# A token mixer's opening with the scale applied first, on TensorE and VectorE, and its output kept by tokens

## The chip, the cores and the metric

One NeuronCore of a Trainium2 chip runs the whole program. The metric is the device time of one execution in microseconds (us); less is better. The kernel before takes 1472.46 us, the median of three runs (1472.07 to 1472.56).

## The reference, cut to what matters

Two transformer blocks work on 256 tokens of width 1024, all in float32. The change touches the first block's way into its token mixer and the way out of it:

```python
ada = jax.nn.silu(c) @ w_ada[l] + b_ada[l]
sh1, sc1, g1, sh2, sc2, g2 = jnp.split(ada, 6, axis=-1)
h = modulate(rms_norm(x, norm1_pre[l]), sh1, sc1)      # h*(1+scale)+shift
y = token_mixer(h, w_in[l], ...)
x = x + g1[:, None, :] * rms_norm(y, norm1_post[l])
h = modulate(rms_norm(x, norm2_pre[l]), sh2, sc2)
y = peer(h, peer_wq[l], peer_subkeys[l], peer_u[l], peer_v[l])
```

In the mixer `proj = h @ w_in` is split into q, k, v, gates and others; q and k go through a causal convolution of four taps and a silu. An RMS norm multiplies each token by one number, the scale multiplies each feature by one number, and the shift adds one number per feature.

## The kernel before, in words

Activations lie by features: `x[128, 8, 256]` has 8 blocks of 128 features, with 256 tokens in the free dimension. Every float32 product is made of three matmuls on rounded halves: `split` (L157) turns 1024 columns of raw weights into a high part `wh` (copy on ScalarE, L165) and a low part `wl` (subtraction, L166, on VectorE or GpSimd). An output block of 128 features takes 24 matmuls of 256 columns: for 8 input blocks, high by high, high by low, low by high (`gemm`, L194). Plain float32 matmuls (fills, sums, transposes) appear as two matmul rows each.

**The opening** follows a hand-written string, `ORD` (L24), one letter per 512 KB load on SyncE's queue. C makes the row `crow` of silu(c) on all partitions; X loads x, sums its squares, and multiplies it by the norm into `u` (L529). Each B (shift) and S (scale) takes a block of `w_ada` and makes 128 numbers of `ada` by one VectorE multiply-and-sum over 1024 columns (`product`, L446). B0 to B7 come first, then S0 to S7; after each S, `A1` is formed (L549), ScalarE applies scale and shift (L551) and rounds to `hh` (L555), and GpSimd makes the low part `hl`. W0 to W5 are the weights of six of the eight q and k blocks. When an `hh` block is there, `some` (L568) runs the matmuls of four outputs (L573); two more outputs follow, and the last two (W6, W7) are loaded in the next list.

**The next list**, `ORD2` (L25): w loads and splits a weight of q or k, q makes its product, u reads one output (`unit_qk`, L600: copy out of PSUM, four taps on VectorE, tanh, gate), v makes a quarter of v (`wide`, L199), l and g the gates. `PV` and `WG` name the splits that GpSimd does. Then a loop over 8 blocks (from L740) makes three products each (`wcxb`) and in their shadow the eight heads, which need the q and k outputs, and two of the later `ada` products each. The program is ordered by priority in the order written, as operands come free, by a planner with its own cost estimates; products of `ada` and the opening's loads keep the order written.

**The mixer's end** (from L826): `acc_k` adds up the output by features in four PSUM banks; then come the squares (ScalarE and VectorE), sums and norm over partitions (L846 to L849), `residual` (L357) with two VectorE operations of 256 columns per block, `scaled` (L338), and the first four products of the next stage (`gemms`, L222). `LA` and `F1` place weight splits and fill matmuls there. **The end of the expert stage** (L1145 to L1182) does the same job by tokens: `acc_tok` (L249) keeps 128 tokens by 512 features per bank, `ended` norms each half with a number per partition, and 16 transposes bring it back.

`NW` (L35) paces the making of expert weights (`weights_of`, L1061) beside the products z 50 to 95; what is left is drained before the next stage starts.

Of the kernel before, what the change touches and what calls it, by code (L numbers as in the profile page):

```python
# [32 lines left out]
LA = ('nnre',(2,3))  # L33
# [5 lines left out]
NZ, NR, NW, ZR, NX, NY = (7, 1.7, 1.4, 50, 1.05, 1.05)  # L39
# [73 lines left out]
def body(ctx: ExitStack, tc: tile.TileContext, a: dict):  # L113
# [243 lines left out]
    def residual(pool_, x, y, r, gain, then=None):  # L357
        for j in range(8):
            u = pool_.tile([128, 256], F32, tag="u", name="u", bufs=2)
            V.scalar_tensor_tensor(out=u, in0=y[:, j, :], scalar=gain[:, j:j + 1], in1=r, op0=ALU.mult, op1=ALU.mult)  # L360
            V.tensor_add(x[:, j, :], x[:, j, :], u)
            if then:
                then(j)
# [68 lines left out]
    with ExitStack() as p1:  # L432
# [3 lines left out]
        crow = m1.tile([128, 1024], F32, name="crow")  # L436
        A.dma_start(out=col, in_=a["cols"])
# [29 lines left out]
        u = big("u", 5)  # L467
        qz = big("qz", 2)
        G.memset(qz, 0.0)
# [9 lines left out]
        banks = [bank(t) for t in ("sc", "num", "den", "ssq", "bc")]  # L479
        psb = bank("psb")  # L480

        early = []

        def load_c():

            c1, t1 = m1.tile([128, 1024], F32, tag="adas", name="c1", bufs=1)[:1], slot_of("t1", 7)[:1, :1024]
            tc.keep_in_program_order(SY.dma_start(out=c1, in_=a["c"]))
            A.activation(t1, c1, AF.Tanh, scale=0.5)
            V.scalar_tensor_tensor(out=c1, in0=t1, scalar=1.0, in1=c1, op0=ALU.add, op1=ALU.mult)
            for n in range(F0):  # L490
                T.matmul(psb[:, :128], lhsT=ones, rhs=ones, start=True, stop=True)
            for i in range(2):
                early[:] = [T.matmul(banks[i], lhsT=ones[:1, :], rhs=c1[:, i * 512:(i + 1) * 512], start=True, stop=True)]
                A.copy(crow[:, i * 512:(i + 1) * 512], banks[i])
# [28 lines left out]
        def load_x():  # L523
            tc.keep_in_program_order(SY.dma_start(out=x, in_=a["xT"].rearrange("p (j t) -> p j t", j=8)))
            with tc.issue_after(early[0].ins):
                sums(m1, banks[4], x, presum(m1, x))
                r1 = norm(m1, banks[4])[0]
# [1035 lines left out]
```

## Time and profile before

| | us |
|---|---|
| median of three runs | 1472.46 |
| the profiled execution | 1472.34 |
| its span in the profile | 1470.3 |
| TensorE busy in the span | 1428.5 |
| VectorE busy | 1152.7 |
| ScalarE busy | 913.8 |
| GpSimd busy | 41.9 |

The profile is of one execution; 2.0 us lie outside its span. TensorE rows are modelled with their pipeline, so a row's length is longer than the pitch at which matmuls follow one another; the pitch is read from start to start. PE is TensorE, PEld its weight loads, DVE is VectorE, ACT is ScalarE, POOL is GpSimd, SP is SyncE.

### The profile page before, as it was taken

What the parts mean: (1) busy time and instruction counts of PE and PEld (TensorE: products, weight loads), DVE (VectorE), ACT (ScalarE), POOL (GpSimd) and SP (SyncE); (2) the same over time, 40 slices, a digit from 0 to 9 for tenths busy, and PEclk for the clock granted to TensorE, in tenths of its full rate; (3) what the DMA queues carried; (4) which work ended last, traced back from release to release, by engine and by line L of the source; (5) the groups of instructions that cost most, each with busy time, mean ns of one, the idle gap of its engine ahead of it and who ended that gap; (6) DMA issues with size and microseconds to landing.
All of it is one profiled execution on the core that took longest, in us unless ns stands there. A gap on an engine that the chain in (4) does not pass through costs nothing.

```text
span 1470.3 us, 27107 instructions
## 1 busy us (share of the span) xinstructions
PE 1428.5 (97%) x10998; PEld 1312.4 (89%) x10998; DVE 1152.7 (78%) x2184; ACT 913.8 (62%) x1288; POOL 41.9 (3%) x30
## 2 busy tenths in 40 slices
PE   5899999999999999999999999999999999999998
PEld 4889999988999999998779997777788899998897
DVE  8988997667999977878999897888855769565554
ACT  3554565446444578887777777787744679554542
POOL 3310000010000000000000000000000000000000
PEclk7999999999999999999999999999999999999999
DMA  9557686453545554453455545555555554255552
GB/s 348 185 190 268 234 345 225 170 171 128 194 151 201 175 178 167 170 172 129 162 173 198 170 151 189 180 173 172 172 176 197 190 171 133 99 193 181 172 174 84
DMA packets 40016, 268.67 MB, mean 183 GB/s; under 512 B 4562, under 2 KB 5330, under 8 KB 9171
## 3 DMA queue, kind: packets, MB, share of 16 engines
q1 hardware_dynamic: 38882, 264.67, 52.0%
q10 hardware_dynamic: 1008, 2.27, 0.5%
q8 instruction: 86, 1.41, 0.4%
q14 instruction: 40, 0.32, 0.1%
HBM read 265.87 MB, written 1.05 MB: 182 GB/s over the span
## 4 chain that ended last, share of the span: by engine, by line
PE 89%; DVE 6%; ACT 3%; DMA 2%; issue 1%; SPq 0%; DVEq 0%; ACTq 0%
PE mm L189 15%; PE mm L191 15%; PE mm L190 15%; PE acc L260 10%; PE acc L261 10%; PE acc L262 10%; PE g L1094 3%; DMA araw<-in_wada_dram 2%; DVE wl L166 1%; PE acc L189 1%; PE acc L191 1%; PE acc L190 1%; ACT wh L165 1%; DVE scr L448 1%; PE mm L225 1%
## 5 line engine op out<-in xcount | busy, mean ns | idle before, releaser
L165 ACT CAST wh<-raw 128x1024 fp32r<-128x1024 f32 x450 | 471.3, 1050 | 428.8 <-PE mm L190 218.4
L166 DVE TENSOR_TENSOR wl<-raw,wh 128x1024 fp32r<-128x1024 f32 x440 | 536.7, 1222 | 161.1 <-ACT wh L165 155.7
L189 PE MATMUL mm<-hh,wh 128*128 128x256 f32 x1816 | 517.4, 285 | 0.0
L191 PE MATMUL mm<-hh,wl 128*128 128x256 f32 x1816 | 511.7, 282 | 0.0
L190 PE MATMUL mm<-hl,wh 128*128 128x256 f32 x1816 | 510.1, 281 | 0.0
L189 PEld LDWEIGHTS mm<-hh,wh 128*128 128x128 f32 x1816 | 342.2, 188 | 2.2
L190 PEld LDWEIGHTS mm<-hl,wh 128*128 128x128 f32 x1816 | 342.8, 189 | 1.0
L191 PEld LDWEIGHTS mm<-hh,wl 128*128 128x128 f32 x1816 | 343.1, 189 | 0.1
L260 PE MATMUL acc<-wh,ah 128*128 128x512 f32 x512 | 205.5, 402 | 0.0
L261 PE MATMUL acc<-wh,al 128*128 128x512 f32 x512 | 202.6, 396 | 0.0
L262 PE MATMUL acc<-wl,ah 128*128 128x512 f32 x512 | 202.3, 395 | 0.0
L1072 ACT COPY o<-os 128x1024 f16<-128x1024 f16 x96 | 197.0, 2052 | 0.2 <-DVE os L1069 0.2
L262 PEld LDWEIGHTS acc<-wl,ah 128*128 128x128 f32 x512 | 96.7, 189 | 22.5
L261 PEld LDWEIGHTS acc<-wh,al 128*128 128x128 f32 x512 | 96.6, 189 | 20.8
L260 PEld LDWEIGHTS acc<-wh,ah 128*128 128x128 f32 x512 | 96.2, 188 | 20.7
L1097 DVE SCALAR_TENSOR_TENSOR z<-g,z 128x256 f32<-128x256 f32 x128 | 51.3, 422 | 44.9 <-PE g L1094 44.4
L1069 DVE TENSOR_TENSOR os<-io,idxT 128x1024 f16<-128x1024 f16 x96 | 66.4, 692 | 25.2 <-ACT o L1072 24.8
L1079 DVE TENSOR_TENSOR og<-o,gT 128x512 f16<-128x512 f16 (+1 forms) x96 | 82.7, 861 | 0.1
L1094 PEld LDWEIGHTS <-o 128*128 128x128 f16 x1536 | 46.4, 96 | 17.6 <-issue 11.9
L448 DVE SCALAR_TENSOR_TENSOR scr<-araw,crow 128x1024 f32<-128x1024 f32 x48 | 60.5, 1260 | 0.9 <-DMA araw<-in_wada_dram 0.6
L1094 PE MATMUL g<-og,o 128*128 128x32 f16 (+1 forms) x1536 | 56.5, 182 | 2.4 <-ACT o L1072 2.4
L268 DVE TENSOR_TENSOR al<-z,ah 128x256 fp32r<-128x256 f32 x128 | 53.5, 420 | 3.1 <-ACT ah L267 3.1
(437 smaller groups left out, 1888.1 us busy)
## 6 DMA issues: line engine op xcount, KB each, us to landing
raw<-in_uT_dram SPq DMA_DIRECT2D x64, 1024.0 KB, 4.9
raw<-in_ev_dram SPq DMA_DIRECT2D x64, 1024.0 KB, 4.9
araw<-in_wada_dram SPq DMA_DIRECT2D x16, 1024.0 KB, 5.2
raw<-in_wup_dram SPq DMA_DIRECT2D x16, 1024.0 KB, 4.9
raw<-in_wdn_dram SPq DMA_DIRECT2D x16, 1024.0 KB, 5.0
raw<-in_wcxb_dram SPq DMA_DIRECT2D x12, 1024.0 KB, 5.1
araw<-in_wada_dram SPq DMA_DIRECT2D x16, 512.0 KB, 9.8
raw<-in_wout_dram SPq DMA_DIRECT2D x8, 1024.0 KB, 4.9
```

The source lines that it names most:

```text
L165: by.copy(wh, raw) if by is A else by.tensor_copy(wh, raw)
L166: last = on.tensor_sub(wl, raw, wh)
L189: T.matmul(ps, lhsT=wh, rhs=xh, start=start, stop=False, skip_group_check=skip)
L190: T.matmul(ps[:, :n], lhsT=wh, rhs=xl, start=False, stop=False, skip_group_check=skip)
L191: return T.matmul(ps, lhsT=wl, rhs=xh, start=False, stop=stop, skip_group_check=skip)
L260: T.matmul(acc[t][c], lhsT=xh[:, ts_], rhs=wh[:, cs], start=first and n == 0, stop=False)
L261: T.matmul(acc[t][c], lhsT=xl[:, ts_], rhs=wh[:, cs], start=False, stop=False)
L262: T.matmul(acc[t][c], lhsT=xh[:, ts_], rhs=wl[:, cs], start=False, stop=last and n == len(steps) - 1)
L448: return V.scalar_tensor_tensor(out=scr, in0=raw, scalar=0.5, in1=crow, op0=ALU.mult, op1=ALU.mult, accum_out=ada[:, j:j + 1])
L1072: A.copy(o1, os.rearrange("p n t -> p t n"))
L1079: V.tensor_tensor(out=og, in0=o2[:, :, None, :].to_broadcast([128, TB, 2, m]), in1=gT[:, ts_, :, None].to_broadcast([128, TB, 2, m]), op=A ...
L1094: T.matmul(ps[:, t], lhsT=o1[:, t, :], rhs=og[:, t, i], start=i == 0, stop=i == 1)
```

## The change

The opening has a new order: scales before shifts. Five scale blocks are made on TensorE: eight float32 matmuls each with the weights as stationary operand and silu(c) broadcast over 128 columns; three stay on VectorE. Seven q and k outputs are made from `x` times the scale (`xh`, `xl`) instead of from `hh`, `hl`: first high by high as soon as scale and weight are there, then the other two products, which carry the shift in two extra columns (258). The norm is multiplied in and the shift's product added when the output is read (`unit_qk`). `hh` and `hl`, which the other products need, are made beside that by VectorE and ScalarE. The sums of squares go to TensorE alone, the row of silu(c) is made by transposing broadcasts. An agenda says after which load each step is issued. GpSimd no longer splits anything in the opening, in v and at the mixer's end. Seven weights stand in the opening; three of the reads move into the later loop (`ORD3`); the first tap of each convolution goes to ScalarE. The mixer's output is kept by tokens in two halves, by the way of the expert stage, whose code becomes `norm_tokens` and `turn_and_add` (10 fills). `NW` goes from 1.4 to 1.5. Lines that the kernel section prints are not repeated here as removed.

```diff
-ORD = "C X B0 B1 W0 B2 B3 W1 B4 B5 W2 B6 B7 W3 F S0 S1 S2 S3 S4 S5 S6 S7 W4 W5 H"
-ORD2 = "w0 u0 u1 q6 u2 w1 v0 u6 u3 q7 v1 l0 u4 u7 v2 g0 u5 v3"
-FL = dict(B4=2,B5=2,W2=2,B6=2,B7=2,W3=2,S0=2)
-F0 = 10
-PV = (1,3,5,7)
-WG = 47
-F1 = (3,8)
+
+ORD = "C S0 X0 S1 X1 W0 S2 S3 W1 S4 W2 S5 W3 S6 S7 B0 W4 B1 W5 B2 W6 B3 B4 B5 B6 B7 W7"
+ORD2 = "u0 u1 q7 v0 u4 v1 l0 u7 u2 v2 g0 v3"
+
+NS = 5
+ORD3 = {0: 5, 2: 6, 4: 3}
...
-NZ, NR, NW, ZR, NX, NY = (7, 1.7, 1.4, 50, 1.05, 1.05)
+NZ, NR, NW, ZR, NX, NY = (7, 1.7, 1.5, 50, 1.05, 1.05)
...
+    def norm_tokens(acc, yt, rt):
+
+        def ended(t, c):
...
+        return ended
+
+    def turn_and_add(yt, turned, gain, then, n):
+
+        for t in range(2):
+            ts_ = slice(t * 128, (t + 1) * 128)
+            for j in range(8):
+                T.transpose(turned[t][j // 4][:, j % 4 * 128:j % 4 * 128 + 128], yt[:, t, j * 128:(j + 1) * 128],
+                            C("ident"))
+            if t == 0:
+                fill(mmt(), n)
+            for j in range(8):
+                V.scalar_tensor_tensor(out=x[:, j, ts_], in0=turned[t][j // 4][:, j % 4 * 128:j % 4 * 128 + 128],
+                                       scalar=gain[:, j:j + 1], in1=x[:, j, ts_], op0=ALU.mult, op1=ALU.add)
+                if t == 1:
+                    then(j)
...
+        pss = [pmm.tile([128, 512], F32, tag="mm", name="mm", bufs=2)[:, :258] for _ in range(2)]
+        rows2 = [bank(t) for t in ("den", "ssq")]
+        scl = bank("psb")
+        pss += [bank("sc", 258), rows2[0][:, :258], bank("num", 258), rows2[1][:, :258], scl[:, :258]]
...
+            b = (t, n // 2)
             if n % 2 == 0:
...
+                if b in (("S", 0), ("S", 3), ("B", 2)):
...
+        def row_of_c():
+            for i in range(2):
+                for k in range(4):
+                    T.matmul(rows2[i][:, k * 128:(k + 1) * 128], lhsT=cs[:, 4 * i + k:4 * i + k + 1].to_broadcast([128, 128]),
+                             rhs=C("ident"), start=k == 0, stop=k == 3, skip_group_check=True)
+                A.copy(crow[:, i * 512:(i + 1) * 512], rows2[i])
...
+        def squares_of(e, j0):
+            for j in range(j0, j0 + 2):
+                sq = m1.tile([128, 256], F32, tag="sq", name="sq", bufs=4)
+                A.activation(sq, x[:, j, :], AF.Square)
+                plan(e + 1, sums_of, sq, j)
+
+        def sums_of(sq, j):
+            for t in range(2):
+                T.matmul(aux[:, 256 + t:257 + t], lhsT=sq[:, t * 128:(t + 1) * 128], rhs=ones[:, 0:1],
+                         start=j == 0 and t == 0, stop=j == 7, skip_group_check=True)
...
+            A.copy(wh, p)
+            ws.append((wh, wl))
+            plan(e + 1, lambda: V.tensor_sub(wl, p, wh.bitcast(F32)))
+            if n < 7:
+                plan(e + 1, first_products, n, None)
+                plan(e + 2, last_products, n, None)
...
+        def load_scale(e, k):
+            if k >= NS:
+                tc.keep_in_program_order(product(adaload(a["wada"][4:], "S", k), 8 + k))
+                plan(e + 1, gain_of, k)
+                plan(e + 2, first_products, None, k)
+                plan(max(e + 3, 13), normed_of, k)
                 return
...
+            raw = adaload(a["wsc"], "S", k)
+            for i in range(8):
+                T.matmul(scl[:, 128 * (k % 4):128 * (k % 4) + 128], lhsT=raw[:, i * 128:(i + 1) * 128],
+                         rhs=cs[:, i:i + 1].to_broadcast([128, 128]), start=i == 0, stop=i == 7, skip_group_check=True)
+            plan(e + 1, gain_of, k)
+            plan(max(e + 3, 13), normed_of, k)
+            plan(e + 2, first_products, None, k)
+
+        def gain_of(k):
+            by_pe = scl[:, 128 * (k % 4):128 * (k % 4) + 1], half
+            s_, w_ = by_pe if k < NS else (ada[:, 8 + k:9 + k], KS("n1pre"))
+            V.scalar_tensor_tensor(out=A1[:, k:k + 1], in0=s_, scalar=w_[:, k:k + 1], in1=one[:, k:k + 1], op0=ALU.mult,
+                                   op1=ALU.add)
+            scaled(x, A1, xh, xl, k)
+
+        def normed_of(k):
+            V.scalar_tensor_tensor(out=u[:, k, :], in0=x[:, k, :], scalar=A1[:, k:k + 1], in1=r1, op0=ALU.mult,
+                                   op1=ALU.mult)
+
+        def load_shift(e, k):
+            product(adaload(a["wada"], "B", k), k)
+            plan(e + 1, shift_of, k)
+            plan(e + 2, last_products, None, k)
+
+        def shift_of(k):
+            V.tensor_add(B1[:, k:k + 1], ada[:, k:k + 1], col[:, bo + k:bo + k + 1])
+            A.copy(xh[:, k, 256:257], B1[:, k:k + 1])
+            V.tensor_sub(xh[:, k, 257:258], B1[:, k:k + 1], xh[:, k, 256:257].bitcast(F32))
+            A.copy(xl[:, k, 256:258], xh[:, k, 256:258])
+            A.activation(hh[:, k, :256], u[:, k, :], AF.Identity, bias=B1[:, k:k + 1])
+            plan(len(ORD.split()) + 2, low_of, k)
+
+        def low_of(k):
+            V.scalar_tensor_tensor(out=hl[:, k, :256], in0=u[:, k, :], scalar=B1[:, k:k + 1],
+                                   in1=hh[:, k, :256].bitcast(F32), op0=ALU.add, op1=ALU.subtract)
...
+        def first_products(n, k):
+
+            if n is None:
+                ready_s.append(k)
+                pairs = [(i, k) for i in ready_w]
+            else:
+                ready_w.append(n)
+                pairs = [(n, i) for i in ready_s]
+            for n, k in pairs:
+                T.matmul(pss[n][:, :256], lhsT=ws[n][0][:, k * 128:(k + 1) * 128], rhs=xh[:, k, :256], start=k == 0,
+                         stop=False, skip_group_check=True)
...
+            for n, k in pairs:
+                for w_, x_ in ((0, xl), (1, xh)):
+                    T.matmul(pss[n], lhsT=ws[n][w_][:, k * 128:(k + 1) * 128], rhs=x_[:, k, :], start=False,
+                             stop=k == 7 and w_ == 1, skip_group_check=True)
...
+        qz = big("qz", 2)
+        G.memset(qz, 0.0)
...
-            V.tensor_scalar(out=out, in0=src[:, 0:256], scalar1=w(0, j), scalar2=None, op0=ALU.mult)
+            A.activation(out, src[:, 0:256], AF.Copy, scale=w(0, j))
...
-            A.copy(pad[:, 3:259], ps)
+            if j < 7:
+                V.tensor_reduce(out=B1[:, j:j + 1], in_=ps[:, 256:258], axis=AX.X, op=ALU.add)
+                V.tensor_mul(pad[:, 3:259], ps[:, :256], r1)
+                A.activation(pad[:, 3:259], pad[:, 3:259], AF.Identity, bias=B1[:, j:j + 1])
+            else:
+                A.copy(pad[:, 3:259], ps)
...
+            if j in ORD3:
+                unit_qk(pss[ORD3[j]], ORD3[j])
...
-                acc_k(acc, (next(co), (mixh[:, k, :256], mixl[:, k, :256])), first=k == 0)
-        acc_k(acc, *[(next(co), (mixh[:, k, :256], mixl[:, k, :256])) for k in (6, 7)], last=True)
-        ssy = mmt(258)
+                acc_tok(acc, (next(co), (mixh[:, k, :256], mixl[:, k, :256])), first=k == 0)
+        acc_tok(acc, *[(next(co), (mixh[:, k, :256], mixl[:, k, :256])) for k in (6, 7)], last=True,
+                then=norm_tokens(acc, yt, rt))
         raws = [load(a["wq"][b]) for b in range(2)]
...
-        residual(m1, x, acc, ry, prm[:, 0:8], lambda j: scaled(x, prm[:, 8:16], hh, hl, j))
+        turned = [[pw.tile([128, 512], F32, name=f"turned{i}") for i in range(2)],
+                  [pacc.tile([128, 512], F32, tag=f"acc{i}", name="turned") for i in range(2)]]
+        turn_and_add(yt, turned, prm[:, 0:8], lambda j: scaled(x, prm[:, 8:16], hh, hl, j), F1)
...
-    r["c"] = n(c)
+    r["c"] = feat(c)
+    r["wsc"] = colchunks(w, [1024 + 128 * i for i in range(6)])
```

## Rows read from the trace of the kernel before

**Rows 1.** Stretches: busy us (and instructions) of each engine, granted clock, DMA share, GB/s.

```profile
30.00:40.00 10.00, 5.30 (x28) 5.30 (x29) 9.79 (x18) 3.77 (x8) 2.11 (x3) 0.55 0.95 346
...
100.00:140.00 40.00, 40.00 (x321) 38.79 (x321) 34.95 (x73) 19.06 (x40) 0.00 (x0) 1.00 0.66 236
140.00:200.00 60.00, 60.00 (x491) 58.76 (x491) 54.70 (x112) 36.44 (x84) 0.00 (x0) 1.00 0.74 265
```

**Rows 2.** Timeline of TensorE, 55 to 63 us: start, length, instruction, idle time before it.

```profile
55.30 0.28 PE L189 MATMUL mm<-hh,wh 128*128 128x256 f32 x1
...
58.15 0.28 PE L208 MATMUL mm<-wh,hh 128*128 128x256 f32 x1
...
62.48 0.39 PE L210 MATMUL mm<-wl,hh 128*128 128x256 f32 x1 [3.93 <-DVE wl L166]
```

**Rows 3.** Groups of TensorE instructions, 30 to 110 us: busy, mean ns, idle before.

```profile
L210 PE MATMUL mm<-wl,hh 128*128 128x256 f32 x64 | 18.9, 296 | 3.9 <-DVE wl L166 3.9
...
L189 PE MATMUL mm<-hh,wh 128*128 128x256 f32 x45 | 12.8, 284 | 0.0
```

**Rows 4.** VectorE and GpSimd in the opening and the next list, from the timeline.

```profile
17.80 9.23 DVE L529 TENSOR_TENSOR u<-x,rr 128x256 f32<-128x256 f32 x8 [0.53 <-ACT rr L336]
18.79 7.62 POOL L166 TENSOR_TENSOR wl<-raw,wh 128x1024 fp32r<-128x1024 f32 x3 [3.88 <-ACT wh L165]
...
28.21 1.23 DVE L448 SCALAR_TENSOR_TENSOR scr<-araw,crow 128x1024 f32<-128x1024 f32 x1
...
29.48 1.23 DVE L448 SCALAR_TENSOR_TENSOR scr<-araw,crow 128x1024 f32<-128x1024 f32 x1
...
33.36 0.22 DVE L549 SCALAR_TENSOR_TENSOR A<-ada,col,one 128x1 f32<-128x1 f32 x1
```

**Rows 5.** The same engine later: splits and taps of the reads.

```profile
54.88 1.23 DVE L597 SCALAR_TENSOR_TENSOR cv<-pad,col,cv 128x256 f32<-128x256 f32 x3
56.05 1.21 DVE L166 TENSOR_TENSOR wl<-raw,wh 128x1024 fp32r<-128x1024 f32 x1
...
58.95 2.34 DVE L595 TENSOR_SCALAR cv<-pad,col 128x256 f32<-128x256 f32 x1
```

**Rows 6.** DMA, 0 to 60 us: GB/s in 40 slices of 1.5 us.

```profile
GB/s 0 165 383 382 261 423 418 418 429 410 426 415 418 429 418 418 423 410 431 85 98 360 380 317 421 429 431 366 11 0 0 0 0 0 0 87 371 393 202 224
```

**Rows 7.** TensorE's plain float32 matmuls, from the timelines: fills at the start, sums, later fills.

```profile
1.08 4.25 PE L491 MATMUL psb<-ones 128*128 128x128 f32 x20 [1.08 <-DVE pad L602]
...
319.81 1.04 PE L313 MATMUL mm<-ones,sq 128*128 128x1 f32 x8
...
321.96 1.95 PE L321 MATMUL spare<-ones 128*128 128x128 f32 x16
```

**Rows 8.** Timeline of the mixer's end.

```profile
319.05 0.28 PE L191 MATMUL acc<-hh,wl 128*128 128x256 f32 x1
...
322.17 4.86 POOL L166 TENSOR_TENSOR wl<-raw,wh 128x1024 fp32r<-128x1024 f32 x2 [237.39 <-PE mm L331]
...
323.36 3.95 DVE L361 TENSOR_TENSOR x<-x,u 128x256 f32<-128x256 f32 x2
...
340.51 0.37 ACT L336 COPY rr<-ss 128x256 f32<-128x256 f32 x1 [1.25 <-PE ss L331]
```

**Rows 9.** Timeline of the expert stage's end.

```profile
1165.63 0.39 PE L262 MATMUL acc<-wl,ah 128*128 128x512 f32 x1
...
1171.79 0.74 PE L224 MATMUL mm<-hh,wh 128*128 128x256 f32 x4 [1.50 <-ACT hh L340]
1172.08 3.26 DVE L341 SCALAR_TENSOR_TENSOR hl<-x,col,hh 128x256 fp32r<-128x256 f32 x8
```

**Rows 10.** Timeline of TensorE where the expert weights are drained.

```profile
682.95 0.64 PE L1094 MATMUL g<-og,o 128*128 128x64 f16 x16 [2.44 <-ACT o L1072]
...
685.18 0.63 PE L261 MATMUL acc<-wh,al 128*128 128x512 f32 x1
685.61 0.63 PE L262 MATMUL acc<-wl,ah 128*128 128x512 f32 x1
```

More of the change, by code (lines that the diff above doesn't have):

```diff
@@ L477, in bct @@
             return bank("bc", 256)
[L479 to L494, printed above, removed]
+        pss = [pmm.tile([128, 512], F32, tag="mm", name="mm", bufs=2)[:, :258] for _ in range(2)]
+        rows2 = [bank(t) for t in ("den", "ssq")]
+        scl = bank("psb")
+        pss += [bank("sc", 258), rows2[0][:, :258], bank("num", 258), rows2[1][:, :258], scl[:, :258]]
+        aux = bank("bc")
+        xh, xl = (slot_of(n, i, F32R)[:, :2064].rearrange("p (j n) -> p j n", j=8) for n, i in (("xh", 6), ("xl", 7)))
+        u = big("u", 5)
+        A1, B1, one, half, cs, ct = (m1.tile([128, 8], F32, name=n) for n in ("A1", "B1", "one", "half", "cs", "ct"))
+        rc = m1.tile([128, 4], F32, tag="rc", name="rc", bufs=1)
+        r1 = m1.tile([128, 256], F32, name="r1")
+        raws = [sp.tile([128, 2048], F32, tag="raw", name="raw", bufs=3) for _ in range(3)]
+        raws.append(None)
+        stage, ws, done, low = {}, [], [], []
         def halfload(raw, src, i):
@@ L514, in adaload @@
                 else:
                     stage[b] = m1.tile([128, 2048], F32, tag="araw", name="araw", bufs=2)
-            raw = halfload(stage[b], src[n // 2], n % 2)
-            warm(f"{t}{n}", raw)
-            return raw
-        raws = [sp.tile([128, 2048], F32, tag="raw", name="raw", bufs=3) for _ in range(3)]
-        ws, more = [], []
[L523 to L527, printed above, removed]
-            for j in range(8):
-                V.tensor_mul(u[:, j, :], x[:, j, :], r1)
@@ L531, in load_w, with plan, load_c @@
-        def load_w(n):
+            return halfload(stage[b], src[n // 2], n % 2)
+        agenda = {}
+        def plan(at, f, *args):
+            agenda.setdefault(at, []).append((f, args))
+        def load_c(e, _):
+            A.activation(ct, cc, AF.Tanh, scale=0.5)
+            V.scalar_tensor_tensor(out=cs, in0=ct, scalar=1.0, in1=cc, op0=ALU.add, op1=ALU.mult)
+            V.tensor_scalar_add(one, col[:, bo + 8:bo + 16], 1.0)
+            V.tensor_mul(one, one, KS("n1pre"))
+            V.tensor_scalar_mul(half, KS("n1pre"), 0.5)
+            for n in range(F0):
+                T.matmul(scl[:, :128], lhsT=ones, rhs=ones, start=True, stop=True)
+            plan(6, row_of_c)
@@ new lines, in norm_of, with load_w @@
+        def norm_of():
+            A.activation(rc[:, 0:2], aux[:, 256:258], AF.Sqrt, bias=epsc, scale=1.0 / D)
+            V.reciprocal(rc[:, 2:4], rc[:, 0:2])
+            for t in range(2):
+                T.matmul(aux[:, t * 128:(t + 1) * 128], lhsT=rc[:, 2 + t:3 + t].to_broadcast([128, 128]), rhs=C("ident"),
+                         start=False, stop=t == 1, skip_group_check=True)
+            A.copy(r1, aux[:, :256])
+        def load_w(e, n):
+            if n == 6:
+                raws[3] = sp.tile([128, 2048], F32, tag="raw", name="raw", bufs=3)
@@ L676, in body @@
             n = int(t[1])
[L677 to L679 removed]
+            if t[0] == "l":
                 wif = m1.tile([128, 8, 72], F32, name="wif")
```

139 lines of the change are left out of this document (49 added, 90 removed).

## The prediction

> **What bounds the kernel now.** I read the stretches first. TensorE is busy without a gap from about 100 us to the mixer's end at 319 us, and VectorE is not [rows 1]; there the end moves only by as much as TensorE starts earlier or waits less. So I count, for each place that the change touches, the time TensorE does not spend on useful matmuls. The useful pitch is 0.119 us for 256 columns: 24 matmuls lie between 55.30 and 58.15 us [rows 2].
>
> The opening: by 110 us TensorE has done 3 x 64 matmuls for v and 3 x 45 for the gemms [rows 3], and by the code 4 x 24 and 2 x 24 for q and k outputs and 24 for gates: 495 x 0.119 = 58.9 us, with some 3 us of small ones 62. So 48 us are lost there, most of it before 47 us. What ends last in it is VectorE: 9.79 of 10 us busy from 30 to 40 us, at a granted clock of TensorE of 0.55 [rows 1]. Part of that is no work: eight `u` multiplications took 9.23 us while GpSimd ran splits, and one tap took 2.34 where three others took 1.23 together [rows 4, 5]. Later TensorE waits 3.93 us for a split [rows 2].
>
> The mixer's end: the last product of the output starts at 319.05, and the next norm's row is only there at 340.88 [rows 8]. The expert weights' drain: 2.44 us of waiting, then matmuls of 512 columns at a pitch of 0.43 us [rows 10].
>
> **The opening, step by step.** Loads: the order is new, but 26 loads of 512 KB (8 S, 2 X, 8 W, 8 B) are 13.6 MB, and at the 420 GB/s of the full slices [rows 6] that is 32.5 us; with some 3 us until the first slices fill, the last shift lands near 35 us, W7 near 36. Two weights that came in the next list now stand ahead of v's loads in SP's queue; I price that at nothing, since v's first load then lands near 41 us (an estimate: 1 MB more at that rate plus the landing), ahead of its use at 54. x comes in two loads, one issue more on SP, also nothing. In the slices of 85 and 98 GB/s SP waited for a buffer; the same waits can come back for the last shifts, but VectorE lies behind by then.
>
> VectorE, from the nearest rows: a product has a pitch of 1.27 us (28.21 to 29.48), a gain 0.22 [rows 4], a split is 1.21 long and taken at 1.15, since rows overlap (three taps of 1.23 end 1.17 after their start, where the split begins), an operation of 256 columns 0.39 to 0.41 [rows 5]. Now: 3 + 8 products 14.0, seven splits 8.0, eight gains 1.7, eight `xl` and eight normed blocks 6.6, eight shifts of two small operations with a round trip to ScalarE between them 3.2 (0.4 each, bounded by 0.3 and 0.7), row and norm 0.8: 34 us. With GpSimd gone from the splits I take them at these lengths (its clearing of `qz` moves behind the opening and may hold one operation; within the bounds). Up to the landing of S5, near 17 us, there is work for only some 5 us; from then each 512 KB brings 1.3 us of DMA time and 1.2 to 2.3 us of VectorE time, so the engine runs through: 17 + 29 = 46 us. TensorE ends the seventh output some 2 us later, 48 us.
>
> TensorE must keep up. A plain matmul of 128 columns is two rows of 0.122 us at full clock, 0.21 at the start (16 in 1.95, 20 in 4.25) [rows 7]. Five scale blocks are 5 x 8 x 0.244 = 9.8 us, 16 sums 32 x 0.13 = 4.2, the row of silu(c) 2.0, and 7 x 24 x 0.119 = 20.0 us of products: 36 us at full clock, from 4.5 us on. That fits under 48 with 7 us to spare; each us at half clock costs half a us of it. Useful work by 48 us is those 20.0, so 28 us are lost.
>
> Then q7 needs W7's split and eight low parts on VectorE, 1.15 + 3.3 = 4.5 us after 46, and the PSUM tile that the read of output 0 frees, 0.6 us: start near 51, loss 3. v's first quarter waits for two splits and the reads of outputs 0 and 1 (2.7 us each), start near 56: loss 2. After that VectorE has 6 splits, three reads and the gates, some 20 us, for 23 us of TensorE; no wait is priced, but 1.5 us for the gates' chain. Loss 28 + 3 + 2 + 1.5 = 34.5 against 48: **-14 us** (rounded up for VectorE's slack; bounds -5 and -23: VectorE done at 55 or at 37 us).
>
> The three reads in the later loop bring 2.7 us each to VectorE and nothing to TensorE, and the first tap moves to ScalarE. VectorE is busy 34.95 of 40 and 54.70 of 60 us there [rows 1], so 10.4 us are free for 3 x 2.7 less eight taps of 0.35 = 5.3. Cover enough on average, not everywhere: **+1** (0 to +4). Behind such a late read stand the splits of `wcxb` and the multiplication that frees one of two PSUM tiles, and TensorE waits for both.
>
> **The mixer's end.** The expert stage's end does the same job by tokens. From its last matmul at 1165.63 to the first of the next stage are 6.2 us, low parts done at 1175.34, 9.7 us after [rows 9]. At the mixer the matmuls then last 64 x 0.12 = 7.7 us, to 13.9; the norm's sums are 12 rows of 0.13, its transposes 4 of 0.122 [rows 7], the copy 0.37 [rows 8], root and reciprocal an estimate of 0.5: 1.6 + 0.5 + 0.4 + 0.5 = 3.0, so the row is there some 17 us after the last product. Before it took 21.8, of which two additions of 0.42 us took 3.95 under a GpSimd split of 4.86 [rows 8]. Sum: **-5** (-2, if ScalarE's copies of weights or GpSimd's sums of squares come between, to -6.5). The accumulation itself has the same columns: nothing.
>
> One rule speaks against it. After the expert stage's 16 transposes (and 20 fill rows) four matmuls of 256 columns took 0.74 us [rows 9], the same as at full clock. The Trainium skill, "TensorE: Matmul & The Clock Gate", Part 4, says of transposes that they do not count as TensorE's work for its clock; by it the 64 products could run at half clock, 6 us more, and this part would cost 1 us. The trace disagrees, so the sum goes by the row.
>
> **NW.** At 1.4 advances per product, 46 products give 64.4 for the 64 that the weights take, so the last block falls at the drain; at 1.5 it comes three products earlier. Gone are 2.44 us and some nine matmuls at 0.43 instead of 0.23 [rows 10], 1.8 us: **-4** (0, if the order keeps a copy of weights ahead of the next stage's first operand, to -4.2).
>
> Sum: -14 + 1 - 5 - 4 = -22. The profiled execution took 1472.34 us (span 1470.3 and 2.0 outside), the median 1472.46; so **1450 us**.
>
> **Rivals.** (1) VectorE finds work earlier and the loads set the opening's pace (shifts done near 38 to 40 us): opening -22, total -30, 1442. For it: the agenda spreads the work by loads; against: the 5 us that are there before 17. Chance 0.2. (2) VectorE, in order, stands behind TensorE's scale blocks in the first 20 us and is done near 54: opening -7, and the later loop +3: total -13, 1459. For it: each gain now waits for eight float32 matmuls, at 0.42 us each at half clock. Chance 0.2. (3) The opening gains nothing, because the planner's order undoes the agenda; with the other two parts half there, 1470. Chance 0.06. (4) Slower: TensorE stays at its lower clock through the opening. Place: scale blocks, sums and products up to the seventh output; price: 36 us become 72, the output ends at 77 instead of 48, +29 on -22: 1479. It decides once it costs over 22 us, that is with about four fifths of those 36 us at the low level (36 + 29.5 from 4.5 on is 70, 22 behind 48). For it: the clock was 0.55 from 30 to 40 us with TensorE 53% busy [rows 1]; against: now TensorE has work of 36 in 44 us. The Trainium skill states in "TensorE: Matmul & The Clock Gate", Part 1, that the throttled state is the default and activity lifts it; the rows of half clock agree. Chance 0.06.
>
> **How the numbers follow.** The forecast has 0.48. The range 1438 to 1463 holds it and most of (1) and (2), some 0.8. A measurement of this kernel tells 0.2%, 3 us, from no change. Slower by more: (4), 0.06; within: most of (3) and the tail of (2), 0.07; faster: the rest, 0.87.
>
> **What would show it.** Right: products of L448 at 1.2 us with no GpSimd beside them; the seventh output done at 46 to 50 us; granted clock near 1 from 20 us on; v's first quarter near 56; the row of the second norm 17 us after the mixer's last product; no 2.44 us wait before the first `acc`. Wrong: VectorE idle between 10 and 30 us behind gains, half clock beyond 20 us, TensorE gaps in the loop of `wcxb` behind VectorE reads, or ScalarE's weight copies inside the norm of the token halves.

## The result and the profile after

The changed kernel takes 1454.64 us, the median of four runs (1452.25 to 1455.17), against 1472.36 us for the kernel before beside it (1472.07 to 1472.56): a ratio of 0.9879, 95% interval 0.9867 to 0.9891. That is 17.7 us less; forecast were 22, to 1450, with a range of 1438 to 1463. The profiled execution took 1454.75 us, its span 1453.0. Repeats of the changed kernel lie within 2.9 us, those of the kernel before within 0.5.

The page of the changed kernel, span and busy time by engine:

```profile
span 1453.0 us, 27094 instructions
...
PE 1429.3 (98%) x10984; PEld 1312.0 (90%) x10984; DVE 1133.2 (78%) x2208; ACT 923.3 (64%) x1322; POOL 7.8 (1%) x11
```

TensorE's busy time is what it was; the idle time went. Four points divide the 17.3 us by which the spans differ; each is a start on TensorE's timeline.

| | before | after | gained up to here |
|---|---|---|---|
| first matmul of the heads | 100.83 | 91.18 | 9.6 |
| end of the mixer's last product (start plus pitch) | 319.17 | 309.67 | 9.5 |
| last `hl` by `wh` matmul of the first product after the second norm (`mmz`) | 353.14 | 339.73 | 13.4 |
| last accumulation of the first expert stage | 1165.63 | 1148.28 | 17.35 |

So the stretch up to the heads gave 9.6 us, the loop with the three late reads nothing, the mixer's end 3.9, `NW` 3.9. "The last `mmz` matmul" means the third of these points from here on; the 24 matmuls with the weights' low part that follow it run at 0.12 us in both kernels. Stretches of the changed kernel, which answer to [rows 1] (busy us and instructions of PE, PEld, DVE, ACT, POOL; granted clock, DMA share, GB/s):

```profile
15.00:20.00 5.00, 4.86 (x33) 4.75 (x33) 1.23 (x1) 2.83 (x6) 0.00 (x0) 0.75 1.02 419
...
30.00:40.00 10.00, 5.20 (x24) 4.69 (x24) 10.00 (x22) 3.19 (x7) 0.00 (x0) 0.56 0.81 270
...
100.00:140.00 40.00, 40.00 (x326) 39.09 (x325) 37.34 (x79) 23.59 (x54) 0.00 (x0) 1.00 0.71 253
140.00:200.00 60.00, 60.00 (x489) 58.71 (x488) 56.16 (x107) 37.75 (x85) 0.00 (x0) 1.00 0.82 294
```

In the first row VectorE has 1.23 us of work in five; from 30 us on it has no gap at all. In the last two TensorE still has none, with VectorE some 3.9 us busier than before: the reads were covered.

The opening on TensorE (start, length, instruction, idle time before it and what ended it):

```profile
1.08 2.93 PE L542 MATMUL psb<-ones 128*128 128x128 f32 x12 [1.08 <-DVE pad L696]
6.09 3.75 PE L606 MATMUL psb<-cs,araw 128*128 128x128 f32 x16 [2.08 <-DMA araw<-in_wsc_dram]
...
16.50 5.45 PE L606 MATMUL psb<-cs,araw 128*128 128x128 f32 x32
...
58.41 0.28 PE L209 MATMUL mm<-wh,hh 128*128 128x256 f32 x1
```

The last row is the start of v. Between it and the heads TensorE is idle for 2.0 us; in the kernel before it was idle for 7.5 us between v's start at 58.15 and the heads, 3.93 of them in [rows 2]. The next longest gap before, and the longest after:

```profile
81.22 0.38 PE L208 MATMUL mm<-wh,hh 128*128 128x256 f32 x1 [2.00 <-ACT v L214]
...
62.74 0.39 PE L209 MATMUL mm<-wh,hh 128*128 128x256 f32 x1 [1.11 <-ACT v L215]
```

The opening on VectorE, which answers to [rows 4, 5]:

```profile
9.88 0.22 DVE L615 SCALAR_TENSOR_TENSOR A<-psb,half,one 128x1 f32<-128x1 f32 x1 [6.46 <-PE psb L606]
...
13.48 0.22 DVE L615 SCALAR_TENSOR_TENSOR A<-psb,half,one 128x1 f32<-128x1 f32 x1 [2.32 <-PE psb L606]
...
21.98 0.34 DVE L615 SCALAR_TENSOR_TENSOR A<-psb,half,one 128x1 f32<-128x1 f32 x2 [5.06 <-PE psb L606]
22.24 1.22 DVE L592 TENSOR_TENSOR wl<-raw,wh 128x1024 fp32r<-128x1024 f32 x1
...
52.90 0.16 DVE L631 TENSOR_TENSOR xh<-B,xh 128x1 fp32r<-128x1 f32 x1
```

VectorE stands 6.46, 2.32 and 5.06 us behind TensorE's scale blocks; the first of these waits holds the landing of S0's load too, for which TensorE itself waited until 6.09. The first block ran with a row every 0.23 us, the second at 11.50 with one every 0.12. That is half clock by the pitch of the rows alone: the profile's granted clock reads 1.00 up to 16 us. The blocks of S2 and S3 began at 16.50 and gave their gains at 21.98. Only then does VectorE run on, and its last shift falls at 52.90. The loads waited too (SyncE's waits from 0 to 30 us: engine, what was waited for, us in total, times, longest):

```profile
SPq L517 <- PE psb L606: 9.1, 2, 7.6
```

A buffer that TensorE's scale blocks still read held a load of `w_ada` for 7.6 us.

The mixer's end, which answers to [rows 8], from the timelines of TensorE, ScalarE and VectorE:

```profile
309.44 0.39 PE L263 MATMUL acc<-wl,hh 128*128 128x512 f32 x1
...
310.54 2.40 PE L322 MATMUL mm<-ones 128*128 128x128 f32 x20
314.35 1.09 PE L376 MATMUL turned<-ca,yt 128*128 128x128 f32 x8 [1.41 <-ACT yt L367]
316.71 0.39 PE L225 MATMUL mm<-hh,wh 128*128 128x258 f32 x1 [1.26 <-ACT hh L341]
...
309.68 1.04 ACT L166 CAST wh<-raw 128x1024 fp32r<-128x1024 f32 x1
...
311.20 1.05 ACT L166 CAST wh<-raw 128x1024 fp32r<-128x1024 f32 x1
...
327.65 0.37 ACT L337 COPY rr<-ss 128x256 f32<-128x256 f32 x1 [0.31 <-PE ss L332]
...
312.28 1.22 DVE L167 TENSOR_TENSOR wl<-raw,wh 128x1024 fp32r<-128x1024 f32 x1
313.42 0.15 DVE L366 RECIPROCAL rt<-rt 128x1 f32<-128x1 f32 x1
```

The row of the second norm is there 18.6 us after the start of the last product (327.65 + 0.37 - 309.44), against 21.8 before and 17 forecast. Inside the second half's norm stand two copies of weights on ScalarE and their subtractions on VectorE (the second is shown, in front of the reciprocal); the first product comes 7.3 us after the last accumulation, not 6.2 as in [rows 9]. The drain of [rows 10] now waits for nothing; matmuls of 512 columns follow at 0.23 us:

```profile
675.47 0.64 PE L1191 MATMUL g<-og,o 128*128 128x64 f16 x16
...
676.26 0.39 PE L262 MATMUL acc<-wh,al 128*128 128x512 f32 x1
676.49 0.39 PE L263 MATMUL acc<-wl,ah 128*128 128x512 f32 x1
```

### The profile page after: what moved, and what is told of

Read it like the earlier page. It is cut to its first block, busy times and chain, and to the rows that moved or that the text cites. A ratio compares the mean times of both kernels' runs of the same rounds, so it can differ in the third digit from the quotient of the medians.

```text
span 1453.0 us, 27094 instructions
## 1 busy us (share of the span) xinstructions
PE 1429.3 (98%) x10984; PEld 1312.0 (90%) x10984; DVE 1133.2 (78%) x2208; ACT 923.3 (64%) x1322; POOL 7.8 (1%) x11
## 4 chain that ended last, share of the span: by engine, by line
PE 90%; DVE 6%; ACT 2%; issue 1%; DMA 0%; DVEq 0%; SPq 0%; ACTq 0%
PE mm L190 15%; PE mm L192 15%; PE mm L191 15%; PE acc L261 11%; PE acc L262 11%; PE acc L263 11%; PE g L1191 3%; DVE wl L167 1%; PE psb L606 1%; DVE scr L471 1%; ACT wh L166 1%; PE mm L226 1%; PE mm L225 1%; PE acc L190 1%; PE acc L192 1%; PE acc L191 1%
## 5 line engine op out<-in xcount | busy, mean ns | idle before, releaser
L166 ACT CAST wh<-raw 128x1024 fp32r<-128x1024 f32 x444 | 465.3, 1050 | 423.7 <-PE mm L191 219.8
L471 DVE SCALAR_TENSOR_TENSOR scr<-araw,crow 128x1024 f32<-128x1024 f32 x43 | 52.4, 1217 | 0.2
```

The source lines that it names most:

```text
L166: by.copy(wh, raw) if by is A else by.tensor_copy(wh, raw)
L471: return V.scalar_tensor_tensor(out=scr, in0=raw, scalar=0.5, in1=crow, op0=ALU.mult, op1=ALU.mult, accum_out=ada[:, j:j + 1])
```

## The experiments

Every experiment is an edit of the changed kernel; "the changed kernel" below means its 1454.64 us. Ratios are to the kernel before, with 95% intervals, which are some 2 us wide to either side. Where less than that matters, the verdict rests on points of the timeline.

### The two parts that stand alone

The pace of the expert weights, put back:

```diff
-NZ, NR, NW, ZR, NX, NY = (7, 1.7, 1.5, 50, 1.05, 1.05)
+NZ, NR, NW, ZR, NX, NY = (7, 1.7, 1.4, 50, 1.05, 1.05)
```

> The changed kernel with NW back at 1.4, nothing else. Theory (the drain of the expert weights cost a wait and a stretch at the low clock): about 4 us slower than the changed kernel, 1458.5, with a wait of some 2.4 us before the first matmuls of the next stage. Rival (the faster pace only moves work, and the gain of the part lies elsewhere): within 1 us of the changed kernel, 1454.6.

Measured: 1458.27 us, 0.9901 (0.9885 to 0.9918). From the last `mmz` matmul to the stage's last accumulation it takes 812.49 us, to the digit what the kernel before takes; the changed kernel takes 808.55. As expected, that is 4 us more. The wait of [rows 10] is back (TensorE's timeline):

```profile
670.07 0.64 PE L1191 MATMUL g<-og,o 128*128 128x64 f16 x16 [2.44 <-ACT o L1169]
```

So `NW` is worth 3.94 us.

The mixer's end of the kernel before, by features, with `residual`, `LA` and `F1` as they were:

```diff
-                acc_tok(acc, (next(co), (mixh[:, k, :256], mixl[:, k, :256])), first=k == 0)
+                acc_k(acc, (next(co), (mixh[:, k, :256], mixl[:, k, :256])), first=k == 0)
...
-        turn_and_add(yt, turned, prm[:, 0:8], lambda j: scaled(x, prm[:, 8:16], hh, hl, j), F1)
+        residual(m1, x, acc, ry, prm[:, 0:8], lambda j: scaled(x, prm[:, 8:16], hh, hl, j))
```

> The changed kernel with the mixer's end as it was before (output by features, GpSimd with two of the weight splits, two VectorE operations per block). Theory (the end by tokens is worth what the two traces show between the last product and the last low part of the next stage's first products): 4 us slower than the changed kernel, about 1458.5, and from the last product of the mixer to the second norm's row about 21.5 us again instead of 18.0. Rival (the end by tokens gives nothing, since its norm waits for ScalarE's weight copies, and the gain comes from the opening alone): within 1 us, 1454.6.

Measured: 1459.85 us, 0.9919 (0.9903 to 0.9936). From the start of the last product to the last `mmz` matmul it takes 33.94 us (before 34.09, changed kernel 30.29). The two additions of [rows 8] that stood under a GpSimd split are back on VectorE's timeline, at their old length; behind them TensorE waits, and then its matmuls of 256 columns follow at 0.215 us up to 324.4 (granted clock 0.53 from 320 to 325 us):

```profile
314.55 3.95 DVE L391 TENSOR_TENSOR x<-x,u 128x256 f32<-128x256 f32 x2
...
319.34 0.58 PE L227 MATMUL mm<-hl,wh 128*128 128x256 f32 x1 [2.00 <-DVE hl L343]
```

So the end by tokens is worth 3.65 us between these points, about what was expected. The last product, too, comes 0.8 us later (310.23, with the heads at 91.22 as in the changed kernel); why is open.

### What sets the opening

Three scale blocks on TensorE and five on VectorE instead of five and three:

```diff
-NS = 5
+NS = 3
```

> Three scale blocks on TensorE and five on VectorE. Theory A (VectorE's total work sets the opening's end, whatever stands before 22 us): two products of 1.27 us more, 2 to 3 us slower, 1457. Theory B (VectorE stands idle until 22 us behind TensorE's scale blocks, so work moved into that idle time costs nothing and frees TensorE of 3.9 us): the last shift up to 3 us earlier, 1452.

Measured: 1455.22 us, 0.9889 (0.9873 to 0.9906): no difference in time. Neither theory's time came. But the last shift came at 51.92 although VectorE had two products more, 2.5 us of work. In the five traces that share the changed kernel's opening (the changed kernel, `NW` put back, the mixer's old end, GpSimd in v, reads put back) it lies between 52.10 and 52.93, so it is 0.2 to 1.0 us earlier here: the two products cost nothing, and more than that this run does not show. The mixer's last product came 1.0 us earlier than in the changed kernel, and that went at the mixer's end, which took 31.57 us instead of 30.29 (see there).

Four shift loads moved among the scale loads, so that VectorE has products to make early:

```diff
-ORD = "C S0 X0 S1 X1 W0 S2 S3 W1 S4 W2 S5 W3 S6 S7 B0 W4 B1 W5 B2 W6 B3 B4 B5 B6 B7 W7"
+ORD = "C S0 X0 S1 X1 B0 W0 S2 B1 W1 S3 B2 W2 S4 B3 S5 W3 S6 S7 W4 B4 W5 B5 W6 B6 B7 W7"
...
-            plan(6, row_of_c)
+            row_of_c()
```

The rest of a shift's work (`hh`, `hl`) is planned after its scale.

> Four of the shift loads stand among the scale loads, and the row of silu(c) is made before the first scale block, while TensorE waits for the load; the full hh follows its shift only when its normed block is there. Theory B (VectorE's idle time before 22 us is what the opening lost against the forecast): the last shift near 47 us instead of 52.9, the kernel 4 to 6 us faster, 1449 to 1451. Theory A (the opening's end is set by TensorE, or by loads, by then): no more than 1 us faster, or slower, since scale blocks come up to 5 us later: 1454 to 1458.

Measured: 1462.13 us, 0.9933 (0.9916 to 0.995), 7.5 us slower than the changed kernel. The expectation failed, and not at the sum that it was about. The row of silu(c), now first, delayed the first gain from 9.88 to 12.67: its 16 matmul rows take from 6.08 to 9.62, at 0.22 us each, in front of the first scale block (TensorE stands until 6.08 in either kernel). And SyncE, whose loads keep the order written, stood in front of buffers whose readers came later; from 7.21 to 22.81 it issued no load (stretches, and SyncE's longest wait for an engine):

```profile
15.00:20.00 5.00, 4.36 (x33) 3.98 (x33) 2.62 (x7) 3.09 (x6) 0.00 (x0) 0.87 0.36 141
20.00:25.00 5.00, 3.84 (x22) 3.43 (x22) 4.45 (x12) 2.38 (x6) 0.00 (x0) 0.79 0.18 43
...
SPq L517 <- DVE scr L471: 7.6, 1, 7.6
```

Where the changed kernel moved 419 and 265 GB/s, this one moved 141 and 43. The last shift fell at 59.34, the heads began at 98.95. So the run does not answer what it was meant to ask; the next two do.

Two scale blocks on TensorE, and the row of silu(c), which VectorE's products need, planned early enough for them:

```diff
-NS = 5
+NS = 2
...
-            plan(6, row_of_c)
+            plan(2, row_of_c)
```

> Two scale blocks on TensorE, six on VectorE, and the row of silu(c) planned four loads earlier, since VectorE needs it sooner; loads in the changed kernel's order. Theory B (VectorE is idle for some 18 of the first 22 us behind TensorE's blocks, and each us by which the last shift comes earlier reaches the heads and the mixer's end): three products of 1.27 us more for VectorE, but its unbroken stretch starts near 16 us instead of 22, so the last shift comes at 49 to 51 us instead of 52.9 and the mixer's last product 2 to 4 us earlier than 309.4. Theory A (VectorE's total is what counts): the last shift at 54 to 57 us, the kernel 2 to 4 us slower.

Measured: 1452.2 us, 0.9861 (0.9845 to 0.9878). VectorE runs on from 15.70 instead of 21.98 and ends its last shift at 49.98 instead of 52.90, with three products more (its timeline):

```profile
15.70 1.23 DVE L592 TENSOR_TENSOR wl<-raw,wh 128x1024 fp32r<-128x1024 f32 x1 [0.45 <-ACT wh L590]
```

6.3 us earlier less three products of 1.27 us is 2.5; 2.9 came. The mixer's last product also comes 2.9 us earlier (306.50). Theory B held.

Ten fills at the start instead of six, so that TensorE has work until the first scale block lands:

```diff
-F0 = 6
+F0 = 10
```

> Ten instead of six fills before the first scale block. If the half clock of the first block (16 rows in 3.75 us) is what holds the opening back: that block ends up to 1.8 us earlier, and so do the gains, the last shift up to 1.8 us earlier. If VectorE's stretch from 22 us is set by the loads and the third and fourth block: last shift at 52.9 within 0.5 us, the kernel the same within 1 us.

Measured: 1452.73 us, 0.9873 (0.9856 to 0.9889). The same 16 rows that took 3.75 us take 2.02, the blocks of S2 and S3 are done at 18.2 instead of 22.0, and the last shift falls at 49.14, 3.8 us earlier (TensorE's timeline):

```profile
1.08 4.61 PE L542 MATMUL psb<-ones 128*128 128x128 f32 x20 [1.08 <-DVE pad L696]
6.53 2.02 PE L606 MATMUL psb<-cs,araw 128*128 128x128 f32 x16 [0.83 <-DMA araw<-in_wsc_dram]
...
14.43 3.73 PE L606 MATMUL psb<-cs,araw 128*128 128x128 f32 x32
```

The expectation had counted the first block alone, 1.8 us. The blocks of S2 and S3 ran faster too, 3.73 us instead of 5.45; the granted clock from 15 to 20 us is 1.00 here and 0.75 in the changed kernel. So 3 to 4 us of VectorE's late start were TensorE's low clock over blocks that VectorE waited for (the last shift falls at 48.87 and 48.97 in two further runs with ten fills, and at 52.10 to 52.93 with six). The mixer's last product also came 3.8 us earlier (305.64); 1.2 of them were lost again at the mixer's end.

### GpSimd and the late reads

Four low parts of v given back to GpSimd, as in the kernel before:

```diff
-PV = ()
+PV = (1, 3, 5, 7)
```

> The changed kernel with four of v's eight low parts on GpSimd again, as before. Theory (GpSimd's splits hold VectorE's instructions with two operands in SBUF for their length): VectorE has single taps or products of 2 us or more again, and the heads start 2 to 5 us later than 91.2 us. Rival (VectorE is relieved of four times 1.15 us while it is the one that is late): the heads start 2 to 4 us earlier.

Measured: 1462.02 us, 0.9923 (0.9906 to 0.9939), 7.4 us slower. The timelines of GpSimd, VectorE and TensorE:

```profile
56.42 2.41 POOL L167 TENSOR_TENSOR wl<-raw,wh 128x1024 fp32r<-128x1024 f32 x1
58.99 2.34 POOL L167 TENSOR_TENSOR wl<-raw,wh 128x1024 fp32r<-128x1024 f32 x1 [0.16 <-ACT wh L166]
...
56.66 2.45 DVE L691 SCALAR_TENSOR_TENSOR cv<-pad,col,cv 128x256 f32<-128x256 f32 x1 [0.62 <-ACT cv L689]
...
59.15 3.66 DVE L691 SCALAR_TENSOR_TENSOR cv<-pad,col,cv 128x256 f32<-128x256 f32 x4
...
64.70 0.58 PE L209 MATMUL mm<-wh,hh 128*128 128x256 f32 x1 [5.28 <-ACT pad L702]
```

A tap that takes 0.4 us elsewhere lasts as long as the split beside it, and one of the next four does again. Five taps take 6.1 us in place of 2, ScalarE's tanh waits for them, the read that frees a PSUM tile stands behind it, and TensorE stands for 5.28 us; from 60 to 70 us its granted clock is 0.69. The heads begin at 97.28 instead of 91.18, while the last shift is no later (52.10). The Trainium skill, "SBUF — State Buffer", "SBUF: two separate sides", says that VectorE and GpSimd share a pair of ports by an exclusive lock, held for a whole instruction; the 2.45 beside the 2.41 us agrees.

The three late reads put back into the list before the loop:

```diff
-ORD2 = "u0 u1 q7 v0 u4 v1 l0 u7 u2 v2 g0 v3"
+ORD2 = "u0 u1 q7 v0 u4 v1 l0 u7 u2 v2 u5 g0 u6 v3 u3"
...
-ORD3 = {0: 5, 2: 6, 4: 3}
+ORD3 = {}
```

> The three reads of q and k outputs that stand in the loop of wcxb go back into the list before it. Theory (the loop has cover: TensorE has no gap there, and the reads in the list delay v's splits on VectorE): 2 to 6 us slower, since VectorE is busy without a gap to 62 us and 2.7 us per read are added before v's last quarter. Rival (VectorE catches up before v's last quarter, so the place of the reads does not matter): within 1 us of the changed kernel.

Measured: 1455.08 us, 0.9887 (0.987 to 0.9904), the same time. The rival held. The heads begin at 90.12, 1.1 us earlier, and the loop takes 0.7 us longer, so that the mixer's last product stands at 309.10 (changed kernel 309.44). Where the reads stand decides nothing for the time: VectorE has room for them in both places.

### The mixer's end

Over these runs the stretch from the mixer's last product to the last `mmz` matmul took one of two lengths: 30.3 us in the changed kernel and with early shifts or reads put back, 31.5 to 31.6 us with `NW` at 1.4, three or two scale blocks, ten fills, or GpSimd in v. The same instructions; what differs is TensorE's clock after the turn (granted from 310 to 315 us: 1.00 in the changed kernel, 0.77 with ten fills). With ten fills at the start (TensorE's timeline):

```profile
310.55 1.09 PE L376 MATMUL turned<-ca,yt 128*128 128x128 f32 x8 [1.41 <-ACT yt L367]
312.91 0.58 PE L225 MATMUL mm<-hh,wh 128*128 128x258 f32 x1 [1.26 <-ACT hh L341]
...
315.43 0.42 PE L226 MATMUL g<-hl,wh 128*128 128x256 f32 x1
315.65 0.42 PE L225 MATMUL g<-hh,wh 128*128 128x258 f32 x1
```

Up to 316.08 fourteen products follow at 0.215 us instead of 0.12. TensorE had been idle twice for 1.3 to 1.4 us around the second turn. The next run covers the first of these gaps, with fifteen fills between the turns instead of ten:

```diff
-F0 = 6
+F0 = 10
...
-F1 = 10
+F1 = 15
```

> Ten fills at the start as in the run before, and 15 instead of 10 fills between the two turns at the mixer's end. Theory: the first products after the turn ran at half clock in some runs (granted 0.77 from 310 to 315 us with ten fills at the start, 1.00 in the changed kernel itself) because TensorE stood idle twice for 1.3 to 1.4 us around the second turn; ten more fill rows cover the first of the two gaps, so the products run at a pitch of 0.12 us, the last accumulation and the first product of the second stage's mmz lie 30.1 us apart instead of 31.5, and the time is 1.3 us under the 1452.7 of ten fills alone: 1451.4. Rival: the fall has another cause than this gap, a stretch of pitch 0.21 us stays, 31.5 us and 1452.7.

Measured: 1451.3 us, 0.9862 (0.9845 to 0.9878); 30.33 us, the clock granted in full (TensorE's timeline):

```profile
306.52 3.51 PE L322 MATMUL mm<-ones 128*128 128x128 f32 x30
310.33 1.09 PE L376 MATMUL turned<-ca,yt 128*128 128x128 f32 x8 [0.30 <-ACT yt L367]
312.69 0.39 PE L225 MATMUL mm<-hh,wh 128*128 128x258 f32 x1 [1.26 <-ACT hh L341]
```

Both further runs with fifteen fills took 30.2 and 30.3 us. The 1.4 us by which the median fell is within the spread; the length of the stretch is not.

The two copies of weights put behind the second half's norm, with ten fills in both places:

```diff
-F0 = 6
+F0 = 10
...
-        cq = chunks(a["wq"], range(8), raws)
+        cq = chunks(a["wq"], range(8), raws, {2: (A, ended_at[0]), 3: (A, ended_at[0])})
```

`ended_at` holds the copy on ScalarE that ends the second half's norm.

> Ten fills at the start, and the two copies of weights that ScalarE made inside the norm of the second half (1.04 us each, with their two subtractions of 1.22 us on VectorE) come behind that norm. Theory: the copies and subtractions stood in the norm's chain, so the second half is normed some 2 us earlier, the first product comes 5.3 us after the last accumulation instead of 7.3, and the time falls by 1.5 to 2 us, to 1451. Rival: VectorE, busy 4.6 to 4.9 of each 5 us there, is what bounds this stretch; the subtractions then stand in front of the low parts or the products wait for the late weights, and the time stays at 1452.7 or rises by up to 1 us.

Measured: 1454.06 us, 0.9881 (0.9865 to 0.9898). The theory fell. The second half is turned 1.6 us earlier than with ten fills alone, counted from the last accumulation, and the first product still comes 7.2 us after it (TensorE's and VectorE's timelines, then the stretch around it):

```profile
308.81 1.04 PE L378 MATMUL turned<-ca,yt 128*128 128x128 f32 x8
312.65 0.58 PE L225 MATMUL mm<-hh,wh 128*128 128x258 f32 x1 [2.80 <-ACT hh L341]
...
309.17 2.36 DVE L167 TENSOR_TENSOR wl<-raw,wh 128x1024 fp32r<-128x1024 f32 x2
```

```profile
310.47:315.47 5.00, 2.82 (x13) 2.82 (x14) 4.88 (x13) 3.38 (x10) 1.30 (x2) 0.72 0.58 195
```

The two subtractions that left the norm now stand on VectorE in front of the second half's additions of `x`, on which `hh` waits; VectorE is busy 4.88 of the 5 us that follow. No run puts the copies behind the additions too.

This run says something of the clock as well. The first gap is covered here, and the stretch still takes 31.46 us, with products at 0.215: the idle time now lies in one piece, 2.80 us. Around the second turn TensorE is idle for 2.67 to 2.80 us in the nine traces with ten fills and for 1.56 to 1.68 in the three with fifteen.

### Together

Two scale blocks, the early row, ten and fifteen fills:

```diff
-NS = 5
+NS = 2
...
-F0 = 6
+F0 = 10
...
-F1 = 10
+F1 = 15
...
-            plan(6, row_of_c)
+            plan(2, row_of_c)
```

> Two scale blocks on TensorE with an early row of silu(c), ten fills at the start, 15 at the mixer's end. Theory: the two remedies of VectorE's late start overlap and add little, because three more products cost VectorE 3.8 us and the full clock gives TensorE's blocks back what they lost: last shift at 48.3 us against 49.1 and 50.0 of the two alone, time 0.9 us under ten and fifteen fills with five blocks, 1450.5. Rival: they add up in full (last shift at 46 us, 1448.5), since the wait for TensorE's blocks and its half clock are separate losses.

Measured: 1450.91 us, 0.9856 (0.984 to 0.9872). The last shift falls at 48.39, against 49.98 and 49.14 with one remedy; in the next run, whose opening is the same, it falls at 49.15. They overlap, as the theory had it: that two blocks add anything to ten fills these traces do not show. A stretch of it:

```profile
15.00:20.00 5.00, 3.94 (x19) 3.84 (x18) 4.71 (x11) 3.92 (x7) 0.00 (x0) 0.50 1.02 415
20.00:25.00 5.00, 3.87 (x14) 2.78 (x12) 5.00 (x11) 1.89 (x4) 0.00 (x0) 0.50 1.03 421
```

TensorE runs at half clock from 15 to 30 us, and it costs little, since VectorE now sets the pace: from its first split to the last shift VectorE takes 34.6 us, and 34.3 in the run with two blocks and six fills, whose granted clock is 0.65 to 0.69 there.

The same with the copies of weights late as well:

```diff
-        cq = chunks(a["wq"], range(8), raws)
+        cq = chunks(a["wq"], range(8), raws, {2: (A, ended_at[0]), 3: (A, ended_at[0])})
```

> Two scale blocks on TensorE with an early row, ten fills at the start, 15 at the mixer's end, and the two late copies of weights behind the second half's norm. If each part keeps what it gives alone, 1.5 to 2 us under the run with the first three: 1449. If VectorE bounds the mixer's end, as that run, 1450.5, or up to 1 us more.

Measured: 1450.81 us, 0.9857 (0.9841 to 0.9874), the same. These two have the lowest medians, 3.8 us under the changed kernel and 21.3 under the kernel before (1472.13 beside them); from ten and fifteen fills alone (1451.3) they do not differ.

## Why the prediction was right in sign and range, and 4.6 us short

The number lies in the range because the range was wide enough for rival (2), which had a chance of 0.2; the path that the forecast itself took for VectorE did not come about.

**The opening: -9.6 us, forecast -14.** One part of the mechanism held: VectorE ends last, and its last shift sets when q7, v and the heads start. In ten of thirteen traces the heads follow it by 38.2 to 38.5 us (52.90 to 91.18 in the changed kernel, 49.14 to 87.40 with ten fills); with early shifts it is 39.6, with reads put back 37.5, with GpSimd in v 45.2. The term that was mis-sized is "17 + 29 = 46 us". The 29 were nearly right: from 21.98 to 52.90 there are 30.9 us, of which VectorE is idle for 1.2. The 17 was wrong. I took the landing of S5 as the start of VectorE's unbroken work, as if the loads set it. Shown instead is rival (2): the gains of S2 and S3 stand behind 32 rows on TensorE until 21.98, the copies and splits stand in order behind them, and held buffers delay the loads. The two runs that shorten TensorE's part in front of VectorE, by fewer blocks or by full clock, each brought the last shift 3 to 4 us forward. My reckoning for rival (2) had the shifts done near 54 and the time at 1459: the 54 held within 1.1 us. The 1459 did not, because v began 5.5 us after the last shift (58.41), where I had 10 (46 to 56), and because the loop lost nothing, where that rival had 3.

Where the gain lies I did not ask, and it is not mainly in front of v. At v's start (58.15 before, 58.41 after) the changed kernel has one product more behind it, 2.9 us: some 2.6 us of gain. The other 7 come between there and the heads, where the kernel before is idle for 7.5 us, with gaps of 3.93 and 2.00, and the changed one for 2.0. With four low parts of v on GpSimd again, 6.1 of the 9.65 us go back, though the last shift stays. So the largest part of this gain that a run shows is that GpSimd no longer splits in v. No run puts the old opening back with the rest as changed, so what the new order and the scale blocks on TensorE give by themselves is open; ten fills and two blocks show what they had left.

"TensorE must keep up" was worked out as a sum, 36 us of work under 48. The sum was kept; its order was not looked at. Each us at half clock was priced at half a us of slack, while what it cost, 3 to 4 us, fell on the blocks for which VectorE waited. The seventh output was done at 55.6 us, not 48.

**The loop: 0, forecast +1.** 9.65 us earlier at the heads, 9.5 at the mixer's last product, and moving the reads back changed nothing.

**The mixer's end: -3.9 us, forecast -5.** The row of the second norm comes 1.6 us later than forecast, and the first product 1.1. The cause that I had named for a smaller gain was found: copies of weights stand inside the second half's norm. But taking them out gained nothing, since their subtractions then stood in front of VectorE's additions. The other cause is the clock. I set aside the rule that speaks against turning by TensorE because the end of the expert stage showed full clock after its transposes. That was right in size and incomplete: none of the runs had all 64 products at half clock, the 6 us; six of nine with ten fills between the turns had a stretch that costs 1.2 us, and none of the three with fifteen. The 3.9 us are read in an execution without the fall; with it, 2.6 are left. The Trainium skill, "TensorE: Matmul & The Clock Gate", Part 4, says that transposes do not count as TensorE's work for its clock in the same way. The runs show a fall that needs no transposes: the mixer's old end has none, and its products follow at 0.215 us from 319.3 to 324.4 behind idle gaps of 1.50 and 2.00 us, as do those of the kernel before from 329.1 to 332.3. What went with the fall in all of them is idle time; whether the transposes add to it no run separates.

**`NW`: -3.94 us, forecast -4.** The wait and the slow matmuls of [rows 10] are gone, and come back with the old value.

Of the signs of right, two are seen: products at 1.22 us and no wait of 2.44 us. Four are not: the seventh output is done at 55.6, not 46 to 50; the clock is 0.56 from 30 to 40 us; v's first quarter is at 58, not 56; the row of the second norm takes 18.6 us, not 17. Of the four signs of wrong three are seen: VectorE idle behind gains, half clock beyond 20 us, ScalarE's copies inside the norm. That GpSimd's splits lengthened VectorE's work was the base of taking products at their short length; eleven products average 1.22 us now, and the splits given back in v cost 7.4 us.

Two more things stay open: why the clock's fall at the mixer's end comes in some runs with the same ten fills and not in others, and whether the rate of the loads sets a floor under VectorE's stretch, which no run reached.

## What to carry to other kernels

When work moves from one engine to another whose total seems to fit, look at what the first engine does next, in its order: a block that the second engine makes in front of it delays everything behind it, and there the second engine's low clock counted in full. Before work is moved out of a chain, read where it will stand in the queue of the engine that is full. And look for the place where a gain arises, not only for its size: here most of it arose after the stretch that the forecast dwelt on.

## What was not expected of the hardware

The clock mattered where another engine waited for TensorE, not where TensorE had most to do. Four fills more at the start (20 rows, 4.61 us, instead of 12 rows, 2.93) made the first scale block 2.02 us long instead of 3.75 and those of S2 and S3 3.73 instead of 5.45, and brought VectorE's last shift 3 to 4 us forward. At the mixer's end, ten fill rows more, placed in an idle gap of 1.4 us, went with full clock in three runs of three, against three of nine without them. And a stretch at 0.50 of the clock for 15 us, from 15 to 30 us in the run with two scale blocks and ten fills, cost next to nothing.
